# A two-layer diffusion block in fp32 on one core: every operand of a matrix product moved to a multiple of 256 bytes

## The chip, the cores and the metric

The kernel runs on one core of a Trainium2 chip. The metric is the device time of one launch in microseconds (us): 2267.54 us as the median of three runs before the change (2266.43 to 2267.88).

## The reference

A backbone of two layers works on 256 latent tokens and 256 context tokens of width 1024. Each layer is a half-step SwiGLU feed-forward block, then four token mixers on one normalised input (grouped attention, a convolution module, differential attention, a Fourier mix), gated and merged, then a second feed-forward block. In the second layer the context stream stops after the mixers' inputs.

```python
def half_ffn(h, shift, scale, gate, g, w1, w3, w2):
    n = modulate(rms_norm(h, g), shift, scale)
    return h + 0.5 * gate * swiglu(n, w1, w3, w2)      # D_FF = 2816
...
for l in range(DEPTH):                                 # DEPTH = 2
    h, hc = half_ffn(h, ...), half_ffn(hc, ...)
    y, y_ctx = token_mixing(n, nc, w_in[l], ...)       # IN_COLS = 7936, W_OUT 1024 x 1024
    h = half_ffn(h + m[:, 5] * y, ...)
    if l < DEPTH - 1:
        hc = half_ffn(hc + mc[:, 5] * y_ctx, ...)
return rms_norm(h, final_g)
```

## The kernel before, in words

Features lie on the 128 partitions and tokens along the free dimension. Latent and context tokens stand side by side, so most products have 512 moving columns; where only the latent stream is left, or where the closing steps take the two streams apart, they have 256.

**Three products for one.** A float32 value is split into a high part of type float32r and the rest, also float32r. `mm3` (L195 to L199) forms one block of a product from three matmuls: weight high by activation high (L197), weight high by activation low (L198), weight low by activation high (L199). In every one the weight block of 128 x 128 is the stationary operand (a weight load, LDWEIGHTS, precedes each matmul) and the activation is the moving one. Only L908 to L910 have it the other way round. The activations are `nh`, `nl` (the normalised input, 8 blocks of 512 columns), `gh`, `gl` (the hidden layer of the feed-forward block, 22 blocks), `yh`, `yl` (the mixers' outputs), and in the attention `kk` and `sq` tiles (L828, L829), which are float32r too. The weights are `hi` and `lo`, cut by `cut` on ScalarE (L182) and VectorE (L183) out of a `raw` chunk of 512 KB, eight blocks, which SyncE's queue loads. A few products keep plain float32 operands: the transposes (L368, L379, L844, L865), the attention's values (L889, L949), the Fourier mix (L757, L768, L769), the modulation (L257, L303). The built program has 11,388 float32r matmuls, 6,452 with 512 columns and 4,936 with 256, and 928 float32 ones.

**Stages.** `run` (L1079 on) goes through the start (`start`, with its own pool `first`), then for each layer `ffn`, `mixing`, `ffn`. In `ffn` the "up" products come first (22 x 2 columns of weights, moving `nh` and `nl`), then the "down" products (moving `gh` and `gl`): six of eight output blocks with 512 columns (L197 to L199, tiles `pr`), the last two stream by stream with 256 columns in `close` (tiles `pr` and `prc`), where the weights of the very last chunks lie in two spare tiles (tiles `w`). In the second layer's last block all down products have 256 columns.

**Where operands lie.** A tile pool places its tiles one after the other, each on a multiple of 32 bytes; pools follow each other in the order in which they are opened: `fix` (for the whole run), `wp` (weights, three buffers each), `tmp` (scratch), then the pool of the stage at hand (`first`, `ffn..`, `mix..`). All partitions have the same layout. So the small tiles at the end of one pool set the place of all that follows. In the program before, `fix` ends with `lam`, `eps` and `zero` (32 bytes each) and `tmp` holds two `rs` tiles and a `warm` tile of 32 bytes; in the mixing pool `cw` has 496 bytes, `qg` and `stat` 32 each. The built program gives these places, as the remainder of the start address by 256, with the float32r matmuls that read them (every row and block of these tiles is 512, 1024 or 2048 bytes long, so all blocks of a tile have its remainder):

| moving operand | its remainder | stationary operand | its remainder | columns | matmuls |
|---|---|---|---|---|---|
| `nh`, `nl`, `yh`, `yl` of layer 0; `hi`, `lo` at L908 to L910 | 64 | `hi`, `lo`; `nh`, `nl` at L908 to L910 | 64 | 512 | 5040 |
| `nh`, `nl` | 64 | `hi`, `lo` | 64 | 256 | 3168 |
| `gh`, `gl` | 160 | `hi`, `lo` | 64 | 512 | 1188 |
| `gh`, `gl` | 160 | `hi`, `lo` | 64 | 256 | 1032 |
| `yh`, `yl` of layer 1 | 192 | `hi`, `lo` | 64 | 256 | 384 |
| `gh`, `gl` | 160 | spare tiles (`w`) | 160 | 256 | 288 |
| `kk` (attention keys) | 192 | `sq` (queries) | 192 | 512 and 256 | 192 |
| `nh`, `nl` | 64 | `hi`, `lo` in pool `first` (the start) | 160 | 512 | 96 |

Each engine goes through its instructions in the order in which they were written or scheduled; the engines wait for each other by semaphores.

Of the kernel before, what the change touches and what calls it, by code (L numbers as in the profile page):

```python
# [10 lines left out]
F32 = mybir.dt.float32  # L11
# [7 lines left out]
L, D, FF = 2, 1024, 2816  # L19
DB, FB = D // 128, FF // 128  # L20
# [4 lines left out]
TAPS = 31  # L25
# [82 lines left out]
class Chunk:  # L108
    def __init__(self, hi, lo):
        self.hi, self.lo = hi, lo  # L110
# [8 lines left out]
class Build:  # L119
    def __init__(self, nc, tc, es, d):  # L120
        self.nc, self.tc, self.d = nc, tc, d
        self.order = []
        self.after = self.region = None
        pool = lambda name, **kw: es.enter_context(tc.tile_pool(name=name, **kw))
        self.fix = pool("fix", bufs=1)
        self.wp = pool("wp", bufs=3)
        self.tmp = pool("tmp", bufs=2)
        self.ps = pool("ps", bufs=1, space=PSUM)
        self.dram = pool("dram", bufs=1, space=bass.MemoryType.DRAM)
        f = self.fix  # L130
        self.small = f.tile([128, N_SMALL], F32, name="small")
        self.const = f.tile([128, EARLY], F32, name="const")
        self.h = f.tile([128, DB, 2 * T], F32, name="h")
        self.nh = f.tile([128, DB, 2 * T], F32R, name="nh")
        self.nl = f.tile([128, DB, 2 * T], F32R, name="nl")
        self.st = f.tile([128, DB, 32], F32, name="st")
        self.mod = [f.tile([128, 72, 2], F32, name=f"mod{l}") for l in range(L)]
        self.lam = [f.tile([128, 4], F32, name=f"lam{l}") for l in range(L)]
        self.eps = f.tile([128, 1], F32, name="eps")
        self.zero = f.tile([128, 1], F32, name="zero")  # L140

    def sm(self, *key):
        o, w = SMALL[key if len(key) > 1 else key[0]]
# [215 lines left out]
    def rstd(self, x, n, count, name, heads=1):  # L359

        nc = self.nc
        ps = self.aux(f"{name}_ps")
        nt = n // 128
        m = nt * heads
        for i in range(nt):
            nc.tensor.transpose(ps[:, 128 * i:128 * i + 128], x[:, 128 * i:128 * i + 128], self.cst("ident"))  # L368
        r = self.tmp.tile([128, 8], F32, tag="rs", name=f"{name}_s", bufs=2)
        nc.vector.tensor_reduce(out=r[:, 0:m], in_=ps[:, 0:n].rearrange("p (m f) -> p m f", m=m), axis=AX.X, op=ALU.add)  # L370
        nc.scalar.activation(out=r[:, 0:m], in_=r[:, 0:m], func=AF.Sqrt, scale=1.0 / count, bias=self.eps)
        nc.vector.reciprocal(out=r[:, 0:m], in_=r[:, 0:m])
        w = self.tmp.tile([128, 512], F32, tag="rstd", name=f"{name}_w", bufs=1)
        nc.vector.tensor_copy(out=w[:, 0:n].rearrange("p (m f) -> p m f", m=m),
                              in_=r[:, 0:m].unsqueeze(2).broadcast_to([128, m, n // m]))

        def turn(ps=ps):
            for i in range(nt):
                nc.tensor.transpose(ps[:, 128 * i:128 * i + 128], w[:, 128 * i:128 * i + 128], self.cst("ident"))  # L379
            return ps[:, 0:n]  # L380

        return turn
# [64 lines left out]
    def project(self, l, m, b, block, n, x, w, h0=None, warm=False):  # L447

        p = self.acc(f"pr{l}{m}{b}")
        for k in range(n):  # L450
            self.mm3(p[:, 0:w], block(b, k), [t[:, 0:w] for t in x(k)], k == 0, k == n - 1)
            if k == n - 1:
                self.epilogue(l, m, b, p, slice(0, w), h0)()
                if warm:
                    t = self.tmp.tile([128, 1], F32, tag="warm", name="warm", bufs=1)
                    self.nc.scalar.activation(out=t, in_=self.ssum[:, 0:1], func=AF.Sqrt)
            if k % 8 == 7 or k == n - 1:
                yield
# [178 lines left out]
    def mixing(self, l, closing):  # L637
# [5 lines left out]
        with self.tc.tile_pool(name=f"mix{l}", bufs=2) as mp:  # L643
            tl = lambda tag, name, bufs, shape=(128, 512), dt=F32: mp.tile(list(shape), dt, tag=tag, name=name,
                                                                            bufs=bufs)
# [20 lines left out]
                return p  # L666


            cw = tl("cw", "cw", 1, (128, 4, TAPS))
            nc.vector.tensor_scalar(out=cw, in0=self.sm("conv_w", l).rearrange("p (i k) -> p i k", k=TAPS),  # L670
                                    scalar1=0.5, scalar2=None, op0=ALU.mult)
            conv_out = [tl(f"cv{i}", f"cv{i}", 1, (128, S, T)) for i in range(4)]
# [150 lines left out]
            def scores(sq, kt, qt, name):  # L823
                keys = ALL if qt < 2 else CTX
                nk = keys.stop - keys.start
                qs = slice(128 * qt, 128 * qt + 128)
                p = self.aux(f"s{name}")
                nc.tensor.matmul(p[:, 0:nk], sq[:, qs], kt[0][:, keys], start=True, stop=False)  # L828
                nc.tensor.matmul(p[:, 0:nk], sq[:, qs], kt[1][:, keys], start=False, stop=True)  # L829
                st = tl("stat", f"st{name}", 4, (128, 2))  # L830
                nc.vector.tensor_reduce(out=st[:, 0:1], in_=p[:, 0:nk], axis=AX.X, op=ALU.max, negate=True)
                e = tl("e", f"e{name}", 4)
                nc.scalar.activation(out=e[:, 0:nk], in_=p[:, 0:nk], func=AF.Exp, bias=st[:, 0:1],
                                     accum_out=st[:, 1:2])
                nc.vector.reciprocal(out=st[:, 1:2], in_=st[:, 1:2])
                return e, st, nk
# [11 lines left out]


            va = tl("va", "va", 1, (128, 4, 128))  # L850
            qg = tl("qg", "qg", 1, (128, 1))
            nc.vector.tensor_scalar(out=qg, in0=self.sm("qk_g", l)[:, 0:1], scalar1=0.125, scalar2=None, op0=ALU.mult)
            ak, aq, ae, at = [], {}, {}, {}

# [19 lines left out]
            def a_scores(j, qt):  # L874
                for a in range(2):
                    e, st, nk = scores(aq[j][a], ak[a], qt, f"a{j}{qt}{a}")
                    scaled(e, nk, st[:, 1:2])
                    ae[j, qt, a] = e, nk
# [17 lines left out]
            lam = self.lam[l]  # L896
# [32 lines left out]
            def c_scores(h, qt):  # L929
                e0, s0, nk = scores(cq[h][0], ck[h][0], qt, f"c{h}{qt}0")  # L930
                e1, s1, nk = scores(cq[h][1], ck[h][1], qt, f"c{h}{qt}1")
                nc.vector.tensor_tensor(out=s1[:, 1:2], in0=s1[:, 1:2], in1=lam[:, 2:3], op=ALU.mult)
                scaled(e1, nk, s1[:, 1:2])
                nc.vector.scalar_tensor_tensor(out=e0[:, 0:nk], in0=e0[:, 0:nk], scalar=s0[:, 1:2], in1=e1[:, 0:nk],
                                               op0=ALU.mult, op1=ALU.add)
                ce[h, qt] = e0, nk
# [230 lines left out]
```

## Time and profile before

| | |
|---|---|
| three runs: median, lowest, highest | 2267.54, 2266.43, 2267.88 us |
| the profiled execution: its own time | 2266.95 us |
| its span from the first to the last instruction | 2265.2 us |
| mean granted TensorE clock | 0.997 |
| VectorE, ScalarE, GpSimd busy | 65%, 43%, 5% of the span |
| 16 DMA engines: hardware queue's share | 42.4%; 322.81 MB in all, mean 143 GB/s |

PE is TensorE's matmul row, PEld its weight loads, DVE VectorE, ACT ScalarE, POOL GpSimd, SP SyncE. A matmul's row has its start and its length; since matmuls are pipelined and their ends are modelled, the next one starts before that length is over. The distance between two starts is therefore what a matmul costs where TensorE has no other wait, and it is read from the times at which the rows start.

### The profile page before, as it was taken

What the parts mean: (1) busy time and instruction counts of PE and PEld (TensorE: products, weight loads), DVE (VectorE), ACT (ScalarE), POOL (GpSimd) and SP (SyncE); (2) the same over time, 40 slices, a digit from 0 to 9 for tenths busy, and PEclk for the clock granted to TensorE, in tenths of its full rate; (3) what the DMA queues carried; (4) which work ended last, traced back from release to release, by engine and by line L of the source; (5) the groups of instructions that cost most, each with busy time, mean ns of one, the idle gap of its engine ahead of it and who ended that gap; (6) DMA issues with size and microseconds to landing.
All of it is one profiled execution on the core that took longest, in us unless ns stands there. A gap on an engine that the chain in (4) does not pass through costs nothing.

```text
span 2265.2 us, 32288 instructions
## 1 busy us (share of the span) xinstructions
PE 2216.1 (98%) x12822; PEld 1915.5 (85%) x12822; DVE 1479.9 (65%) x2432; ACT 964.6 (43%) x1513; POOL 117.7 (5%) x124
## 2 busy tenths in 40 slices
PE   6999999999999999999999999999999999999998
PEld 4888889888888788888888898888889898998998
DVE  6788874794778645556565545665537889775554
ACT  4323223455557633342222232223224777754443
POOL 0000000000000112110000010000001000121000
PEclk9999999999999999999999999999999999999999
DMA  8566663311222232334544424454534333454553
GB/s 323 184 202 202 207 214 117 119 66 65 75 75 75 75 103 93 112 112 153 163 161 156 155 82 145 158 167 149 165 115 170 122 121 122 139 181 164 180 184 131
DMA packets 92742, 322.81 MB, mean 143 GB/s; under 512 B 9904, under 2 KB 15280, under 8 KB 91952
## 3 DMA queue, kind: packets, MB, share of 16 engines
q1 hardware_dynamic: 92592, 320.76, 42.4%
q8 instruction: 100, 1.64, 0.3%
q14 instruction: 50, 0.41, 0.1%
HBM read 315.48 MB, written 5.24 MB: 142 GB/s over the span
## 4 chain that ended last, share of the span: by engine, by line
PE 87%; DVE 9%; ACT 3%; issue 1%; DMA 0%; POOL 0%; DVEq 0%; SPq 0%; ACTq 0%; POOLq 0%
PE p L198 12%; PE p L199 12%; PE p L197 12%; PE pr L199 7%; PE pr L198 6%; PE pr L197 6%; PE g L197 3%; PE g L198 3%; PE g L199 3%; DVE cv L699 2%; DVE lo L183 2%; PE b L197 2%; PE b L198 2%; PE b L199 2%; PE ao L889 1%
## 5 line engine op out<-in xcount | busy, mean ns | idle before, releaser
L182 ACT ACTIVATE hi<-raw 128x1024 fp32r<-128x1024 f32 x430 | 454.6, 1058 | 885.7 <-issue 250.1
L183 DVE TENSOR_TENSOR lo<-raw,hi 128x1024 fp32r<-128x1024 f32 x422 | 526.2, 1248 | 293.1 <-ACT hi L182 286.9
L197 PE MATMUL p<-nh,hi 128*128 128x512 f32 (+1 forms) x1456 | 521.7, 358 | 2.4 <-ACT nh L409 1.3
L199 PE MATMUL p<-nh,lo 128*128 128x512 f32 (+1 forms) x1456 | 520.9, 358 | 2.5 <-DVE lo L183 2.5
L198 PE MATMUL p<-nl,hi 128*128 128x512 f32 (+1 forms) x1456 | 521.2, 358 | 1.2 <-DVE nl L416 1.1
L325 DVE SCALAR_TENSOR_TENSOR prods<-raw,cond 128x1024 f32<-128x1024 f32 x240 | 289.1, 1222 | 191.5 <-DMA raw<-wst 188.6
L197 PEld LDWEIGHTS p<-nh,hi 128*128 128x128 f32 x1456 | 276.6, 190 | 43.8 <-ACT nh L409 2.2
L199 PEld LDWEIGHTS p<-nh,lo 128*128 128x128 f32 x1456 | 276.6, 190 | 42.9 <-DVE lo L183 3.7
L198 PEld LDWEIGHTS p<-nl,hi 128*128 128x128 f32 x1456 | 276.6, 190 | 41.5 <-DVE nl L416 2.1
L199 PE MATMUL pr<-gh,lo 128*128 128x512 f32 (+1 forms) x656 | 231.4, 353 | 0.0
L198 PE MATMUL pr<-gl,hi 128*128 128x512 f32 (+1 forms) x656 | 229.4, 350 | 0.0
L197 PE MATMUL pr<-gh,hi 128*128 128x512 f32 (+1 forms) x656 | 228.4, 348 | 0.0
L197 PE MATMUL g<-nh,hi 128*128 128x512 f32 (+1 forms) x512 | 174.9, 342 | 0.0
L199 PE MATMUL g<-nh,lo 128*128 128x512 f32 (+1 forms) x512 | 173.4, 339 | 0.0
L198 PE MATMUL g<-nl,hi 128*128 128x512 f32 (+1 forms) x512 | 172.6, 337 | 0.0
L699 DVE SCALAR_TENSOR_TENSOR cv<-yp,cw,cv 128x512 f32<-128x512 f32 (+1 forms) x240 | 148.7, 620 | 4.8
L198 PEld LDWEIGHTS pr<-gl,hi 128*128 128x128 f32 x656 | 123.2, 188 | 19.4
L197 PEld LDWEIGHTS pr<-gh,hi 128*128 128x128 f32 x656 | 123.6, 188 | 18.0
L199 PEld LDWEIGHTS pr<-gh,lo 128*128 128x128 f32 x656 | 123.1, 188 | 17.0
L197 PEld LDWEIGHTS g<-nh,hi 128*128 128x128 f32 x512 | 97.0, 189 | 10.5 <-issue 0.6
L199 PEld LDWEIGHTS g<-nh,lo 128*128 128x128 f32 x512 | 97.0, 189 | 10.4 <-issue 0.2
L198 PEld LDWEIGHTS g<-nl,hi 128*128 128x128 f32 x512 | 97.0, 190 | 9.9 <-issue 0.2
(427 smaller groups left out, 3415.7 us busy)
## 6 DMA issues: line engine op xcount, KB each, us to landing
raw<-wst SPq DMA_DIRECT2D x556, 512.0 KB, 3.4
adaraw<-wst SPq DMA_DIRECT2D x3, 2048.0 KB, 17.1
adaraw<-wst SPq DMA_DIRECT2D x8, 512.0 KB, 7.4
cond<-cond SPq DMA_DIRECT2D x3, 1024.0 KB, 4.8
h<-h SPq DMA_DIRECT2D x2, 1024.0 KB, 7.9
adaraw<-wst SPq DMA_DIRECT2D x2, 1024.0 KB, 10.6
parked<-h SPq DMA_DIRECT2D x8, 256.0 KB, 3.9
h<-parked SPq DMA_DIRECT2D x8, 256.0 KB, 3.1
```

The lines of the kernel that those rows point to most:

```text
L182: self.nc.scalar.activation(out=hv, in_=r, func=AF.Copy)
L183: getattr(self.nc, low).tensor_tensor(out=lv, in0=r, in1=hv.bitcast(F32), op=ALU.subtract)
L197: mm(out, w[0], x[0], start=start, stop=False)
L198: mm(out, w[0], x[1], start=False, stop=False)
L199: mm(out, w[1], x[0], start=False, stop=stop)
L325: nc.vector.scalar_tensor_tensor(out=products[:, s], in0=r, scalar=1.0, in1=cond[:, s], op0=ALU.mult, op1=ALU.mult, accum_out=self.mod[l][ ...
L699: nc.vector.scalar_tensor_tensor(out=o, in0=x, scalar=wk, in1=o, op0=ALU.mult, op1=ALU.add)
L889: nc.tensor.matmul(o[64 * a:64 * a + 64, 0:128], va[:, k0 + k, 64 * a:64 * a + 64], at[j, qt][a][:, 128 * k:128 * k + 128], start=k == 0, ...
```

## The change

Sizes and places of tiles alone. A pool `tiny` is opened ahead of `fix` and takes the `rs` and `warm` tiles; the two loops over dummy tiles only fix their order. In `fix` the small tiles come first, `zero` is widened to 128 bytes, and with them in front `const`, `st`, `h`, `nh` and `nl` begin on multiples of 256 bytes. In the mixing pool `cw`, `stat` and `qg` are widened to 512, 64 and 256 bytes (four `stat` tiles make 256), and views of the old size are used.

In the built program after the change every float32r operand in the table above, moving and stationary, has the remainder 0; so have the float32 operands of the other products, but for every other block of `st`, whose blocks are 128 bytes long (remainder 128). The number, order and shape of the instructions on every engine, and every semaphore that they wait for or raise, are those of before: both programs have the same 18,608 instructions, apart from the addresses. The scratch and raw tiles move with the others (for instance `raw` from 64 to 0, `temp` tiles from 128 to 0). Line numbers grow by 4 from `sm` on.

```diff
         pool = lambda name, **kw: es.enter_context(tc.tile_pool(name=name, **kw))
+        self.tiny = pool("tiny", bufs=1)
         self.fix = pool("fix", bufs=1)
...
         f = self.fix
+        for i in range(2):
+            self.tiny.tile([128, 8], F32, tag="rs", name=f"rs{i}", bufs=2)
+        self.tiny.tile([128, 1], F32, tag="warm", name="warm", bufs=1)
+        self.lam = [f.tile([128, 4], F32, name=f"lam{l}") for l in range(L)]
+        self.eps = f.tile([128, 1], F32, name="eps")
         self.small = f.tile([128, N_SMALL], F32, name="small")
+        self.mod = [f.tile([128, 72, 2], F32, name=f"mod{l}") for l in range(L)]
+        self.zero = f.tile([128, 32], F32, name="zero")[:, 0:1]
         self.const = f.tile([128, EARLY], F32, name="const")
+        self.st = f.tile([128, DB, 32], F32, name="st")
         self.h = f.tile([128, DB, 2 * T], F32, name="h")
         self.nh = f.tile([128, DB, 2 * T], F32R, name="nh")
         self.nl = f.tile([128, DB, 2 * T], F32R, name="nl")
-        self.st = f.tile([128, DB, 32], F32, name="st")
-        self.mod = [f.tile([128, 72, 2], F32, name=f"mod{l}") for l in range(L)]
-        self.lam = [f.tile([128, 4], F32, name=f"lam{l}") for l in range(L)]
-        self.eps = f.tile([128, 1], F32, name="eps")
-        self.zero = f.tile([128, 1], F32, name="zero")
...
-        r = self.tmp.tile([128, 8], F32, tag="rs", name=f"{name}_s", bufs=2)
+        r = self.tiny.tile([128, 8], F32, tag="rs", name=f"{name}_s", bufs=2)
...
-                    t = self.tmp.tile([128, 1], F32, tag="warm", name="warm", bufs=1)
+                    t = self.tiny.tile([128, 1], F32, tag="warm", name="warm", bufs=1)
...
-            cw = tl("cw", "cw", 1, (128, 4, TAPS))
+            cw = tl("cw", "cw", 1, (128, 4 * TAPS + 4))[:, 0:4 * TAPS].rearrange("p (i k) -> p i k", k=TAPS)
...
-                st = tl("stat", f"st{name}", 4, (128, 2))
+                st = tl("stat", f"st{name}", 4, (128, 16))[:, 0:2]
...
-            qg = tl("qg", "qg", 1, (128, 1))
+            qg = tl("qg", "qg", 1, (128, 64))[:, 0:1]
```

## The prediction

> **What bounds the kernel now.** I read the page's busy times first, then the chain of work that ended last, then PE's waits, and then the distances between the starts of matmuls in the timeline.
>
> ```profile
> PE 2216.1 (98%) x12822; PEld 1915.5 (85%) x12822; DVE 1479.9 (65%) x2432; ACT 964.6 (43%) x1513; POOL 117.7 (5%) x124
> ...
> PE 87%; DVE 9%; ACT 3%; issue 1%; DMA 0%; POOL 0%; DVEq 0%; SPq 0%; ACTq 0%; POOLq 0%
> ...
> PE n_ps L368 <- DVE ssum L248: 18.1, 2, 13.2
> PE n_ps L379 <- DVE n_w L374: 3.6, 5, 1.3
> ```
>
> TensorE is busy 98% of the span and makes 87% of the chain. Its longest waits are at the start (18.1 us for the first sums of squares); all others together are some 24 us. So the time is the sum over the matmuls, each at its distance to the next start. The change touches addresses alone, so the question is whether that distance depends on where operands lie. The trace of before holds a natural experiment: the feed-forward block's up and down products have the same shapes, but the moving operand lies at 64 in one and at 160 in the other (remainders by 256, from the table above). This is the first block of layer 1, up products, then down products:
>
> ```profile
> L197 PE MATMUL p<-nh,hi 128*128 128x512 f32 x328 | 127.6, 389 | 0.0
> L198 PE MATMUL p<-nl,hi 128*128 128x512 f32 x328 | 127.6, 389 | 0.0
> L199 PE MATMUL p<-nh,lo 128*128 128x512 f32 x328 | 127.6, 389 | 0.0
> ...
> 1360.57 0.40 PE L197 MATMUL p<-nh,hi 128*128 128x512 f32 x1
> ...
> 1583.41 0.39 PE L199 MATMUL p<-nh,lo 128*128 128x512 f32 x1
> 1583.63 0.40 PE L197 MATMUL pr<-gh,hi 128*128 128x512 f32 x1
> ...
> 1675.81 0.40 PE L199 MATMUL pr<-gh,lo 128*128 128x512 f32 x1
> ...
> L199 PE MATMUL pr<-gh,lo 128*128 128x512 f32 x132 | 52.7, 399 | 0.0
> L198 PE MATMUL pr<-gl,hi 128*128 128x512 f32 x132 | 52.0, 394 | 0.0
> L197 PE MATMUL pr<-gh,hi 128*128 128x512 f32 x132 | 51.8, 392 | 0.0
> ```
>
> Both stretches are free of waits (last column 0.0). Up: 3 x 328 = 984 matmuls from 1360.57 to 1583.41, 222.84 us over 983 distances, **226.7 ns** each. Down: 396 matmuls from 1583.63 to 1675.81, 92.18 over 395, **233.4 ns** each. The weights lie at 64 in both. So 6.7 ns of a down matmul come with a moving operand at 160 beside a weight block at 64. Row by row the down distances repeat with the triple:
>
> ```profile
> 320.40 0.39 PE L197 MATMUL pr<-gh,hi 128*128 128x512 f32 x1
> 320.63 0.39 PE L198 MATMUL pr<-gl,hi 128*128 128x512 f32 x1
> 320.87 0.40 PE L199 MATMUL pr<-gh,lo 128*128 128x512 f32 x1
> 321.10 0.39 PE L197 MATMUL pr<-gh,hi 128*128 128x512 f32 x1
> ```
>
> Three matmuls take 0.70 us, 233.3 ns each, the third (0.87 to 1.10, then on) as dear as the others: a rate, not one stall. Now 256 columns:
>
> ```profile
> 1331.02 0.28 PE L197 MATMUL prc<-gh,w 128*128 128x256 f32 x1
> ...
> 1333.42 0.28 PE L199 MATMUL prc<-gh,w 128*128 128x256 f32 x1
> ...
> 2190.54 0.28 PE L198 MATMUL p<-nl,hi 128*128 128x256 f32 x1
> 2190.66 0.28 PE L199 MATMUL p<-nh,lo 128*128 128x256 f32 x1
> ...
> 2191.14 0.28 PE L197 MATMUL pr<-gh,hi 128*128 128x256 f32 x1
> ...
> 2254.37 0.28 PE L199 MATMUL pr<-gh,lo 128*128 128x256 f32 x1
> ...
> L198 PE MATMUL pr<-gl,hi 128*128 128x256 f32 x176 | 49.8, 283 | 0.0
> L199 PE MATMUL pr<-gh,lo 128*128 128x256 f32 x176 | 49.7, 282 | 0.0
> ```
>
> The first pair spans 20 distances with both operands at 160: 2.40 us, 120.0 ns. The last pair spans 528 matmuls (three groups of 176) with 160 beside 64: 63.23 us over 527, also 120.0. The two rows in between, at 64 beside 64, are 0.12 apart. With 256 columns the place doesn't count in any pair that occurs.
>
> From 226.7 at 512 columns and 120.0 at 256 a column costs 106.7 / 256 = 0.417 ns, so a fixed part of 13.3 ns stands on top of the columns (226.7 - 213.3), and 20.0 in the down products. The 6.7 is the difference of two rates that I can see; whether the 13.3 has to do with place too is the large unknown of this change, since no float32r operand lies at 0 or 128 now.
>
> What speaks to it is the attention in the mixing, where moving and stationary operand lie at 192 together, with a stretch at 64 and 64 on both sides:
>
> ```profile
> 650.64 0.39 PE L198 MATMUL bg<-nl,hi 128*128 128x512 f32 x1
> 650.87 0.40 PE L199 MATMUL bg<-nh,lo 128*128 128x512 f32 x1
> 651.10 0.39 PE L828 MATMUL sc<-ck0h,cq 128*128 128x512 f32 x1
> 651.33 0.39 PE L829 MATMUL sc<-ck0l,cq 128*128 128x512 f32 x1
> 651.56 0.39 PE L828 MATMUL sc<-ck0h,cq 128*128 128x512 f32 x1
> 651.78 0.40 PE L829 MATMUL sc<-ck0l,cq 128*128 128x512 f32 x1
> 652.02 0.39 PE L197 MATMUL ba<-nh,hi 128*128 128x512 f32 x1
> 652.25 0.39 PE L198 MATMUL ba<-nl,hi 128*128 128x512 f32 x1
> 652.47 0.39 PE L199 MATMUL ba<-nh,lo 128*128 128x512 f32 x1
> ```
>
> From 650.87 to 652.25 there are six distances, 1.38 us, some 20 ns more than six times 226.7, for one way in (64 to 192) and one way out. Between the two, from 651.33 to 651.78, it is 0.45 for two distances: the old rate. So 192 beside 192 runs like 64 beside 64, and the price falls due where the places differ. I read this as two streams, the running matmul's and the next weights', that fit together when both start at the same place and disturb each other when they don't. Then only the difference of the places counts, and after the change it is zero everywhere.
>
> **The change part by part.** Instructions, order and waits are those of before; nothing is added.
>
> 1. *`gh`, `gl` from 160 to 0, weights from 64 to 0, 512 columns.* 3 x 396 = 1188 matmuls in three blocks, at 233.4 - 226.7 = 6.7 ns: **8.0 us**. All of it on PE without a wait. What would be late next is the weights:
>
> ```profile
> 0.00:56.00 56.00, 36.09 (x425) 27.59 (x426) 34.74 (x70) 25.09 (x33) 0.20 (x4) 1.00 0.87 326
> 273.50:365.90 92.40, 92.40 (x397) 74.33 (x396) 63.68 (x95) 23.34 (x25) 0.00 (x0) 1.00 0.63 205
> ```
>
> In the first such stretch, the second line here (columns: window, length, PE, PEld, DVE, ACT, POOL, clock, DMA share, GB/s; the first line is the start, used below), VectorE is busy 63.7 of 92.4 us, ScalarE 23.3, the DMAs 63%: 2.7 us less per stretch uncovers nothing.
>
> 2. *The changes of place in the mixing go.* The program has 102 neighbours among float32r matmuls whose places differ; at 20 ns for a pair of them, and nothing at 256 columns, between 0 and 1.0 us. I take **0.7**, near the row above.
>
> 3. *The start, `nh` at 64 beside weights at 160.* 96 matmuls; if each pays the same 6.7 ns it is 0.6 us, but PE waits there for ScalarE and VectorE (18.1 us above), and a faster matmul before a wait gains nothing. Between 0 and 0.6; I take **0.3**.
>
> 4. *256 columns*: 4936 matmuls at 120.0 at every pair of places. Nothing.
>
> 5. *ScalarE's, VectorE's and GpSimd's operands and the DMAs' targets* move by 64 to 128 bytes. No row shows a price of place there. They lie beside PE, except at the start and the end; the DMAs' part at the start is bounded by its 87% share in the first 56 us, and a percent of these would be 0.5 us. I take 0, and up to 1 us either way.
>
> Sum: 8.0 + 0.7 + 0.3 = 9.0 us. Against the profiled execution, 2266.95 us (1.75 more than its span of 2265.2), that is **2258.0 us**; the median, 2267.54, lies 0.6 above that execution.
>
> The Trainium skill, "TensorE: Matmul & The Clock Gate", section "Step-by-step: what each phase is for", says that TensorE has two independent read ports and that loading the next weights takes no read bandwidth from the running matmul. By that rule the place of one operand against the other could not matter, and the sum would be 0. The trace differs, 233.4 against 226.7 ns.
>
> **The rivals.**
>
> *A: the fixed 13.3 ns is a price of place too.* If each operand read that doesn't begin on a large enough boundary costs extra, 64, 160 and 192 all pay and only 0 would not. For it: 13.3 ns is 32 columns' time, 128 bytes, exactly what a read shifted by 64 would touch more if memory were read in pieces of 128 bytes, at both widths. Against it: under such a price 160 and 64 should cost the same with 512 columns, and 64, 160 and 192 behave alike only when paired alike. At most it frees 11,388 x 13.3 = 152 us, and 8 for the first step: 2107. Half of it, for instance at one of the widths, gives 2267 - 76 - 8 = 2183. VectorE's 63.7 us in 92.4 leaves room for that. The same page of the Trainium skill, section "Wait — 56ns, not 53.3ns?", gives a floor of about 2.5 ns above the columns for back-to-back matmuls; worked out as an estimate from it, 10.8 x 11,388 + 8 makes 2136, and no row here has reached that floor at this rate.
>
> *B: no change.* The 6.7 ns belong to `gh` and `gl` for another reason (their distance from each other, the order of buffers) and stay. For it: only one pair of long 512-column stretches shows them. Against it: the attention's rows, and the start at 64 beside 160, where undisturbed distances are as long:
>
> ```profile
> 55.15 0.39 PE L197 MATMUL p<-nh,hi 128*128 128x512 f32 x1
> 55.38 0.40 PE L198 MATMUL p<-nl,hi 128*128 128x512 f32 x1
> 55.62 0.39 PE L199 MATMUL p<-nh,lo 128*128 128x512 f32 x1
> ```
>
> (0.47 us for two, 235 each, with the moving operand at 64 and the weights at 160.) It gives 2267.
>
> *C: slower.* With everything at 0, both streams of every matmul start in the same piece of memory. If that is a bad meeting where 64 and 64 was a good one, the 5040 matmuls that now run at 226.7 pay what the down products pay, 6.7 ns: 34 us, 2301. It decides as soon as the common place costs them 9.0 us / 5040 = 1.8 ns each. For it: place 0 is untested. Against it: 64, 160 and 192, each paired with itself, cost the same.
>
> **How the numbers follow.** Forecast 0.73, A 0.14, B 0.08, C 0.05. About 0.2%, 4.5 us, is what a measurement here can tell from no change: faster means under 2263.0. The forecast with all its bounds lies between 2267 - 8.0 - 1.0 - 0.6 - 1 = 2256 and 2267 - 8.0 + 1 = 2260; I widen it to 2252 to 2262 for what I didn't see of the steps after float32 products. The range takes in B, up to 2268: 0.73 + 0.08 = 0.81. Faster 0.73 + 0.14 less a little for a smaller gain, 0.86; same 0.09; slower 0.05.
>
> **What would show it.** In the down products the three groups should come to 389 ns of length (from 399, 394 and 392) and distances of 226.7, their 396 matmuls to 89.8 us; up products should stay at 226.7, and 256 columns at 120.0. The distances around the attention should lose their 0.23 to 0.24. If the up products' distances shrink, A holds, and the forecast's reading of the fixed part is wrong; if they grow, C; if the down products keep 233, B.

## The result

| | before | after |
|---|---|---|
| median of 5 runs (lowest to highest), us | 2267.54 (2266.43 to 2267.95) | 2259.19 (2257.51 to 2261.28) |
| ratio of the times, 95% interval | | 0.9964 (0.995 to 0.9979) |
| profiled execution, its span, us | 2266.95, 2265.2 | 2257.51, 2255.7 |

The kernel got faster by 8.35 us in the medians and by 9.4 in the profiled executions. 2258.0 had been predicted, between 2252 and 2268. In another set of runs on one chip the changed kernel came to 2258.6 against 2265.64, a ratio of 0.9969 (0.9958 to 0.9981).

First the page of the changed kernel (busy times and the chain) and PE's longest wait, in the places of those shown of before:

```profile
PE 2206.8 (98%) x12822; PEld 1915.0 (85%) x12822; DVE 1478.4 (66%) x2432; ACT 964.2 (43%) x1513; POOL 117.4 (5%) x124
...
PE 87%; DVE 8%; ACT 3%; issue 1%; DMA 0%; POOL 0%; DVEq 0%; SPq 0%; ACTq 0%; POOLq 0%
...
PE n_ps L372 <- DVE ssum L252: 17.7, 2, 12.8
```

TensorE's busy time went from 2216.1 to 2206.8 us, 9.3 less, with the same 12,822 matmul rows (a float32 product can have two). The waits stand where they stood, and VectorE's and ScalarE's busy times changed by 1.5 and 0.4 us. So what was gained lies in the matmuls' own rate.

The changed kernel's timeline, PE alone, at the edges of the up and the down products of the first block of layer 1:

```profile
1352.36 0.40 PE L201 MATMUL p<-nh,hi 128*128 128x512 f32 x1
...
1575.20 0.39 PE L203 MATMUL p<-nh,lo 128*128 128x512 f32 x1
1575.43 0.39 PE L201 MATMUL pr<-gh,hi 128*128 128x512 f32 x1
...
1664.96 0.39 PE L203 MATMUL pr<-gh,lo 128*128 128x512 f32 x1
```

Up: 222.84 us over 983 distances, 226.7 ns, as before. Down: 89.53 us over 395, **226.7 ns** where it had been 233.4. Their groups in that window (matmuls alone, each shape apart) have one length now:

```profile
L201 PE MATMUL pr<-gh,hi 128*128 128x512 f32 x132 | 51.3, 389 | 0.0
L202 PE MATMUL pr<-gl,hi 128*128 128x512 f32 x132 | 51.3, 389 | 0.0
L203 PE MATMUL pr<-gh,lo 128*128 128x512 f32 x132 | 51.3, 389 | 0.0
```

389 ns stands in each row, where it had been 392, 394 and 399. Now 256 columns in the changed kernel's timeline: the first and last row of a group of `yh` and `yl` in layer 1's mixing that ran without a wait, then of the last block's down products:

```profile
1974.70 0.28 PE L201 MATMUL b<-yh,hi 128*128 128x256 f32 x1
...
1977.46 0.28 PE L203 MATMUL b<-yh,lo 128*128 128x256 f32 x1
...
2181.24 0.28 PE L201 MATMUL pr<-gh,hi 128*128 128x256 f32 x1
...
2244.47 0.28 PE L203 MATMUL pr<-gh,lo 128*128 128x256 f32 x1
```

and the same `yh` group in the timeline of the kernel before:

```profile
1985.64 0.28 PE L197 MATMUL b<-yh,hi 128*128 128x256 f32 x1
...
1988.38 0.28 PE L199 MATMUL b<-yh,lo 128*128 128x256 f32 x1
```

The last block: 63.23 us over 527 distances, 120.0 ns, as before. The `yh` group (24 matmuls, 23 distances): 2.76 us now, 120.0 each, and 2.74 before, 119. With the moving operand at 192 beside weights at 64 these products had been a little *faster*; being laid alike cost them 1 ns each. This pair stands in the table of places ahead of the prediction, and its rate had not been read.

Matmul by matmul (both profiles have the same 12,822 rows in the same order), the distances between starts changed as follows: the 1188 down products of 512 columns by -7.97 us, the start's products (64 beside 160) by -0.55, `yh` at 256 columns by +0.30, the other products in the first layer's mixing, the attention's among them, by about -0.3; the first matmul started 0.4 earlier. A further -0.6 us is no gain of the change: it comes from stretches at half the granted clock, shown in the last section. The profile of before has one near 980 us that this one lacks (-1.5 us here), while the one near 2050 us is twice as long in this one (+1.0).

### The profile page after: what moved, and what is told of

It is laid out like the page before. It is cut to its first block, busy times and chain, and to the rows that moved or that the text cites. A ratio compares the mean times of both kernels' runs of the same rounds, so it can differ in the third digit from the quotient of the medians.

```text
span 2255.7 us, 32288 instructions
## 1 busy us (share of the span) xinstructions
PE 2206.8 (98%) x12822; PEld 1915.0 (85%) x12822; DVE 1478.4 (66%) x2432; ACT 964.2 (43%) x1513; POOL 117.4 (5%) x124
## 4 chain that ended last, share of the span: by engine, by line
PE 87%; DVE 8%; ACT 3%; issue 1%; DMA 0%; POOL 0%; DVEq 0%; SPq 0%; ACTq 0%; POOLq 0%
PE p L203 12%; PE p L202 12%; PE p L201 12%; PE pr L202 6%; PE pr L203 6%; PE pr L201 6%; PE g L201 3%; PE g L202 3%; PE g L203 3%; DVE cv L703 2%; DVE lo L187 2%; PE b L201 2%; PE b L202 2%; PE b L203 2%; PE ao L893 1%
```

## The experiments

Three theories stood. **S**, the forecast's: two streams, and only the difference between the place of the moving operand and that of the weights (remainders by 256) counts. **P**, rival A: each operand pays for its own place, in pieces of 64 bytes or more. **G**, rival B: the 6.7 ns are the hidden layer's own. In the edits below a tile in front shifts those that follow it.

**1. Both at 64.** The kernel before, with one tile ahead of `gh`, so that `gh`, `gl` and the spare weight tiles move from 160 to 64, where the other weights are. Nothing lies at 0.

```diff
         with self.tc.tile_pool(name=f"ffn{l}{j}", bufs=1) as pool:
+            pool.tile([128, 40], F32, name="pad")
             gh = pool.tile([128, FB, w], F32R, name="gh")
```

> The layout of before with one tile of 160 bytes put ahead of gh in the feed-forward pools: gh, gl and the spare weight tiles lie at 64 instead of 160, beside weights at 64; nothing else moves and nothing is a multiple of 256. Theory S (only the difference between the places of the running matmul's moving operand and of the weights loaded beside it counts): down products with 512 columns at 226.7 ns, 8.0 us less than before, 2259.5. Theory P (each operand pays for its own place where that is no multiple of 64 bytes): the same 226.7 and 2259.5. Rival G (the 6.7 ns belong to gh and gl whatever their place): 233.4 ns, 2267.5. A price that only multiples of 256 are free of: 233.4 ns, 2267.5.

2259.04 us (2256.92 to 2261.89, 7 runs) against 2266.65, ratio 0.9969 (0.9958 to 0.9979). Its timeline, first and last down product of that block:

```profile
1579.74 0.39 PE L197 MATMUL pr<-gh,hi 128*128 128x512 f32 x1
...
1669.28 0.39 PE L199 MATMUL pr<-gh,lo 128*128 128x512 f32 x1
```

89.54 us over 395, 226.7 ns. One tile of 160 bytes does what the whole change does (2259.04 and 2259.19), and no multiple of 256 is needed. G falls: the same buffers in the same order lost the 6.7 ns by a change of place alone. S and P had both foreseen this.

**2 and 3. Six other differences.** The changed kernel, with `gh`, `gl` pushed on by another amount in each feed-forward block; the weights stay at 0. The second of the two has 160, 192, 224 and 128 in place of these four numbers.

```diff
+            pad = {(0, 0): 32, (0, 1): 64, (1, 0): 128, (1, 1): 32}[l, j]
+            pool.tile([128, pad // 4], F32, name="pad")
             gh = pool.tile([128, FB, w], F32R, name="gh")
```

> The changed layout with a tile ahead of gh whose size differs from block to block: gh and gl lie at 32 in the first feed-forward block, at 64 in the second, at 128 in the third, at 32 in the last (256 columns); all weights stay at 0. Theory S: every one of the three 512-column stretches costs more than 226.7 ns, about 230 to 237 as at a difference of 96; the last stays at 120.0. Theory P: 233.3 at 32, 226.7 at 64 and 128. Rival G: 226.7 in all three. Time by S some 2265 to 2267, by P 2261 to 2262.

> As the run before, with gh and gl at 160, 192 and 224 in the first three feed-forward blocks and at 128 in the last; weights at 0. Theory S: all three stretches above 226.7 ns; if the two streams' meeting repeats every 256 bytes, 160, 192 and 224 need not cost what 96, 64 and 32 cost. Theory P: 233.3 at 160 and 224, 226.7 at 192. Rival G: 226.7 in all three.

2261.02 and 2264.79 us, one run each. The timeline of the first, from the first to the last down product of 512 columns of each block (32, 64, 128), and within the 64 block a stretch of 72 matmuls of 256 columns:

```profile
272.47 0.40 PE L201 MATMUL pr<-gh,hi 128*128 128x512 f32 x1
...
364.64 0.40 PE L203 MATMUL pr<-gh,lo 128*128 128x512 f32 x1
...
1213.98 0.40 PE L201 MATMUL pr<-gh,hi 128*128 128x512 f32 x1
...
1304.41 0.39 PE L203 MATMUL pr<-gh,lo 128*128 128x512 f32 x1
...
1328.30 0.28 PE L201 MATMUL prc<-gh,hi 128*128 128x256 f32 x1
...
1336.34 0.28 PE L203 MATMUL prc<-gh,lo 128*128 128x256 f32 x1
...
1577.91 0.40 PE L201 MATMUL pr<-gh,hi 128*128 128x512 f32 x1
...
1670.07 0.39 PE L203 MATMUL pr<-gh,lo 128*128 128x512 f32 x1
```

Over 395 distances: 92.17 us for 32, 233.3 ns; 90.43 for 64, **228.9**; 92.16 for 128, 233.3. The stretch of 256 columns at 64: 8.04 us over 71, **113.3**. The other, 160, 192 and 224:

```profile
274.27 0.40 PE L201 MATMUL pr<-gh,hi 128*128 128x512 f32 x1
...
366.81 0.39 PE L203 MATMUL pr<-gh,lo 128*128 128x512 f32 x1
...
1216.35 0.39 PE L201 MATMUL pr<-gh,hi 128*128 128x512 f32 x1
...
1308.52 0.39 PE L203 MATMUL pr<-gh,lo 128*128 128x512 f32 x1
...
1582.23 0.40 PE L201 MATMUL pr<-gh,hi 128*128 128x512 f32 x1
...
1674.40 0.40 PE L203 MATMUL pr<-gh,lo 128*128 128x512 f32 x1
```

92.54, 92.17 and 92.17 us: 234.3, 233.3 and 233.3 ns. Every difference but 0 and 64 costs 6.6 ns or more. P in pieces of 64 bytes falls, since 128 and 192 are multiples of 64 and pay. S had missed too: it expected 230 to 237 ns at 64 as well, and 2265 to 2267 us for the first of the two runs, which took 2261.02. What neither theory had: at 256 columns every one of these differences was faster than equal places (the table in the last section, from stretches of 72 to 528 matmuls); that gain, 2.5 us, and the cheap block at 64 put the first run below S's time.

**4. Everything at 32.** The changed kernel with one small tile 32 bytes longer, so that all float32r operands lie at 32.

```diff
-        self.zero = f.tile([128, 32], F32, name="zero")[:, 0:1]
+        self.zero = f.tile([128, 40], F32, name="zero")[:, 0:1]
```

> The changed layout with 32 bytes more ahead of const: every operand of a matrix product, moving and stationary, lies at 32, none at a multiple of 64. Theory S: all as in the changed kernel, 226.7 and 120.0 ns, 2258 to 2260. Theory P: every matmul with 512 columns pays 6.7 ns or twice that (moving and weights), 6452 x 6.7 = 43 us or more: 2302 or slower. A price that only multiples of 256 are free of: slower than the changed kernel by at least the 9 us, 2267 or more.

2257.09 us (2255.3 to 2259.22, 5 runs), ratio to the kernel before 0.9958 (0.9944 to 0.9971). Its timeline at the same edges:

```profile
1354.05 0.40 PE L201 MATMUL p<-nh,hi 128*128 128x512 f32 x1
...
1576.89 0.39 PE L203 MATMUL p<-nh,lo 128*128 128x512 f32 x1
1577.12 0.39 PE L201 MATMUL pr<-gh,hi 128*128 128x512 f32 x1
...
1666.65 0.39 PE L203 MATMUL pr<-gh,lo 128*128 128x512 f32 x1
```

222.84 us over 983 and 89.53 over 395: 226.7 ns both. The common place makes no difference, at 32 as at 0 and 64. This ends P as stated here, and rival A, which the unchanged up products had already ruled out, with it.

**5. A difference of 64 nearly everywhere.** The changed kernel with `hi` and `lo` at 192 and the moving operands at 0, so that the difference is 64 again, with other places.

```diff
         self.nl = f.tile([128, DB, 2 * T], F32R, name="nl")
+        self.wp.tile([128, 48], F32, tag="pad", name="pad", bufs=1)
+        self.tmp.tile([128, 16], F32, tag="pad", name="pad2", bufs=1)
```

> The changed layout with hi and lo moved to 192 and everything else left at multiples of 256, so that nearly every matmul reads its moving operand 64 bytes past the weights' place (by 256). Theory S with the map of the runs before: 512 columns at 228.9 instead of 226.7 ns (6132 matmuls, +14 us; the 192 of L912 to L914 at 233.3, +1.3 us), 256 columns at 117.9 instead of 120.0 (some 4600 matmuls, -10 us), or at 113.3 if they settle as in one short stretch of that map (-31 us): between 2241 and 2265. Theory P (each operand pays alone for a place that is no multiple of 64): nothing changes, 2258 to 2260.

2259.05 us (2253.94 to 2260.42, 4 runs), ratio 0.9961 (0.9947 to 0.9974), the changed kernel's time. Its timeline, first and last up product, then the first and the last down product of 512 columns:

```profile
1359.08 0.39 PE L203 MATMUL p<-nh,hi 128*128 128x512 f32 x1
...
1584.08 0.39 PE L205 MATMUL p<-nh,lo 128*128 128x512 f32 x1
1584.31 0.39 PE L203 MATMUL pr<-gh,hi 128*128 128x512 f32 x1
...
1674.72 0.39 PE L205 MATMUL pr<-gh,lo 128*128 128x512 f32 x1
```

225.00 over 983 and 90.41 over 395: 228.9 ns each, the rate that 64 beside 0 had shown. So it is the difference by 256 that counts. At 256 columns it had 117.8 in the long stretches and 113.3 in some short ones. Matmul by matmul against the changed kernel, where no wait interfered, 512 columns lost 13.1 us and 256 columns gained 12.6: they cancel.

**6. Equal places for 512 columns, 64 apart for 256.** What experiments 2 to 5 point to: from the first product of the second layer's mixing on, where nearly all products have 256 columns, `nh` and `nl` are used 64 bytes further on; the last block's `gh`, `gl` and the second mixing's `yh`, `yl` lie at 64; the weights stay at 0. Some small tiles change places to make room.

```diff
+        wide = [f.tile([128, 2 * T * DB + 16], F32R, name="nh")]
...
+        wide.append(f.tile([128, 2 * T * DB + 64], F32R, name="nl"))
+        at = lambda o: [t[:, o:o + 2 * T * DB].rearrange("p (b t) -> p b t", b=DB) for t in wide]
+        (self.nh, self.nl), self.shifted = at(0), at(16)
...
+        if (l2, which) == (1, 1):
+            self.nh, self.nl = self.shifted
...
+            if (l, j) == (1, 1):
+                pool.tile([128, 16], F32, name="pad")
...
+                    if first:
+                        tl("pad1", "pad1", 1, (128, 16))
```

> The changed layout, with a difference of 64 bytes only where the products have 256 columns: in the second layer nh and nl are used 16 columns further on from the mixing's first product to the end (2592 matmuls with 256 columns), gh and gl of the last block lie at 64 (528), and so do yh and yl of the second mixing (384); weights stay at 0, and the 512-column products of the other stages keep equal places. Theory S: 3504 matmuls gain 2.1 ns (7.5 us) or, settled as in the short stretch, 6.7 ns (23 us), and 192 with 512 columns lose 2.3 to 6.7 ns (0.9 us): 2251 down to 2236, faster than the changed kernel. If the gain of the map was an accident of two short stretches: 2258 to 2260.

2251.78 us (2251.08 to 2254.78, 5 runs), ratio to the kernel before 0.9936 (0.9922 to 0.995). Run again on one chip with the changed kernel:

> The kernel with a difference of 64 bytes in the second layer's 256-column products once more, beside the changed kernel on the same chip. Theory S with the measured 117.8 ns for 3504 matmuls: 6 to 8 us below the changed kernel, 2250 to 2254. If its lead was the chip's: the same time as the changed kernel.

> The changed kernel itself, on the chip and beside the runs of the kernel before that the next kernel has too. Theory S as before: 2257 to 2261, 512 columns at 226.7, 256 at 120.0 ns. If the drop of the first measurement were one chip's or one session's: nearer to 2267.

2251.14 us (2250.64 to 2253.29) beside 2258.6 (2256.29 to 2260.91): 7.5 us faster than the changed kernel, 14.5 than the kernel before. The timeline of this kernel's first profiled execution (2251.08 us), the last block's down products:

```profile
2176.40 0.28 PE L204 MATMUL pr<-gh,hi 128*128 128x256 f32 x1
...
2238.47 0.28 PE L206 MATMUL pr<-gh,lo 128*128 128x256 f32 x1
```

62.07 us over 527, 117.8 ns, where equal places gave 63.23. Matmul by matmul between the two profiled executions on one chip, the 3,383 products of 256 columns that no wait disturbed got 7.6 us shorter, 2.25 ns each, and the 192 of 512 columns that use the shifted `nh`, `nl` (half of them as the stationary operand) paid 0.8. So some 6.8 of the 7.5 us are shown to be the places'. The rest need not be: the changed kernel's profile has three stretches at half the clock there and this one's has one.

**7. A smaller weight load.** Is the fixed 13.3 ns of an equally laid matmul the price of the load beside it? The changed kernel with half the weight columns in the second product, which halves that load.

```diff
-        mm(out, w[0], x[1], start=False, stop=False)
+        mm(out[0:64], w[0][:, 0:64], x[1], start=False, stop=False)
```

> The changed kernel with the second product of each three (weight high by activation low) cut to the first 64 of its 128 stationary columns: that part of the product is left out for the upper 64 outputs. Its weight load reads 256 bytes instead of 512, while the first product runs. If the fixed 13.3 ns is time that the weight load takes from the running matmul: the distance from the first product to the second falls by some 6.7 ns (to 220 at 512 columns), the other two stay at 226.7, or the same share in the sum of the three. If it is a cost of changing weights or of starting a matmul: all three stay at 226.7.

2263.11 us, one run. The loads of the down products by group, and the timeline of the down products of 512 and of 256 columns:

```profile
L201 PEld LDWEIGHTS pr<-gh,hi 128*128 128x128 f32 x656 | 123.1, 188 | 17.1
...
L202 PEld LDWEIGHTS pr<-gl,hi 128*64 128x64 f32 x656 | 88.7, 135 | 16.9
```

```profile
1589.79 0.39 PE L201 MATMUL pr<-gh,hi 128*128 128x512 f32 x1
...
1680.55 0.39 PE L203 MATMUL pr<-gh,lo 128*128 128x512 f32 x1
...
2189.03 0.28 PE L201 MATMUL pr<-gh,hi 128*128 128x256 f32 x1
...
2250.51 0.28 PE L203 MATMUL pr<-gh,lo 128*128 128x256 f32 x1
```

The load got shorter, 135 ns from 188. The matmuls of 512 columns got *slower*: 90.76 us over 395, 229.8 ns; those of 256 faster: 61.48 over 527, 116.7. Both expectations missed the 512 columns. By product the distances of 512 columns were 228.9, 230.4 and 230.0 ns, so the first did not fall and the others did not stay. Where no wait interfered, 512 columns lost some 17 us in all and 256 gained some 14, which is how the time came out above the changed kernel's. So the fixed part is not in proportion to the load. The edit also halves the output rows of the second product, so which of the two made 512 columns slower isn't shown.

**8. One of the two weight tiles aside.** Which load disturbs which matmul? The changed kernel with `lo` alone at 96 and all else at 0, so that one of the three products meets another difference, 160 by 256 (0 less 96).

```diff
+                if not self.padded and pool is None:
+                    self.padded = self.wp.tile([128, 24], F32, tag="pad", name="pad", bufs=1)
                 lo = (pool or self.wp).tile([128, 8, 128], F32R, tag="lo", name=f"lo{i}", bufs=bufs)
```

> The changed layout with lo alone moved to 96; hi and all moving operands stay at 0. Theory S (running matmul against the weights loaded beside it): the distance from the second product to the third grows, since lo is loaded while the second runs; over the three the mean rises by a third to all of 6.7 ns. If what counts is a matmul's own pair of operands: the distance from the third product to the next first grows. If neither, 226.7 in all.

2286.48 us, one run. Its timeline, the down products of 512 columns:

```profile
1604.72 0.40 PE L205 MATMUL pr<-gh,hi 128*128 128x512 f32 x1
...
1696.59 0.39 PE L207 MATMUL pr<-gh,lo 128*128 128x512 f32 x1
```

91.87 us over 395, 232.6 ns, against 226.7; the 528 of 256 columns in the last block came to 119.0. The rise is not confined to one matmul in three: by line the distances after the three products are 233.3, 231.7 and 232.8. The mean rose by 5.9 ns, within what S allowed, but all three distances grew where each theory had named one. This experiment doesn't tell whether a matmul is disturbed by the weights for itself or by those for the next; it shows that one ill-placed operand in three slows the whole stream. That made this the slowest kernel of the study: against the changed kernel the products of 512 columns lost 33.8 us, and those of 256 gained 3.8.

## Why the prediction was right

- **Term 1, the down products, 8.0 us.** Right in cause and size: 7.97 us measured, 233.4 to 226.7 ns. Experiment 1 gets it with these places alone changed. Nothing was late behind them; the columns 0.0 say that no wait was uncovered.
- **"Only the difference of the places counts."** Shown for 512 columns: equal places at 0, at 32 and at 64 all give 226.7; 64 beside 0 and 0 beside 192 both give 228.9. Two more differences were met from two places each: 160 as 160 beside 0 (experiment 3, 234.3) and as 64 beside 160 (the start of the kernel before, 234.2 over 81 undisturbed distances); 192 as 192 beside 0 (experiment 3) and as 0 beside 64 (experiment 6), 233.3 both. The price is no single one, though: 2.2 ns at 64, 6.6 to 7.6 elsewhere.
- **"The running matmul's and the next weights'" streams disturb each other.** Not shown. In most stretches a matmul's own weights and the next ones have the same place; experiment 8 sets them apart and all three distances rose, and with half a load (experiment 7) the distance beside it did not get shorter at 512 columns.
- **Term 2, the mixing, 0.7 us.** Too large: some 0.3 in the whole of the first layer's mixing. The changed kernel's timeline at the attention:

```profile
646.95 0.39 PE L203 MATMUL bg<-nh,lo 128*128 128x512 f32 x1
647.17 0.39 PE L832 MATMUL sc<-ck0h,cq 128*128 128x512 f32 x1
...
648.08 0.39 PE L201 MATMUL ba<-nh,hi 128*128 128x512 f32 x1
648.30 0.39 PE L202 MATMUL ba<-nl,hi 128*128 128x512 f32 x1
```

Six distances are 1.35 us, where 1.38 had been, so the mechanism is there; but most of the 102 neighbours stood at a wait or had 256 columns, and the price of one place doesn't hold for all.
- **Term 3, the start, 0.3 us.** 0.55 measured, near the upper bound of 0.6: of its 96 matmuls, 82 had distances below 250 ns before and after, and they lost 6.5 ns each, 0.53 us. The wait for ScalarE and VectorE was not what set them.
- **Term 4, "with 256 columns the place doesn't count in any pair that occurs": wrong.** `yh` at 192 beside 64 had 119 ns, and lost 0.30 us by the change. The reading took two pairs for all. That it stayed small is luck: equal places, which the change makes universal, are the dearest or tied for it at 256 columns.
- **Term 5, the other engines.** VectorE's and ScalarE's busy times changed by 0.1% of their own or less; nothing of it shows in the time.
- **The sum.** 9.0 us predicted, 9.4 between the profiled executions, 8.35 between the medians, 7.0 in the second set of runs. The terms measured make 7.97 + 0.3 + 0.55 - 0.30 = 8.5; the rest of the profiled 9.4 is the first matmul's earlier start, 0.4, and the stretches at half the clock, 0.6. Term 1 carries the forecast. The small terms, 1.0 us foreseen and 0.55 measured, were each off, in part against each other.
- **The rivals.** A fell to the up products, unchanged at 226.7, and to experiment 4; B to experiment 1; C's "place 0 is untested" to the same 226.7.

The Trainium skill, "TensorE: Matmul & The Clock Gate", section "Step-by-step: what each phase is for", has the weight load take no read bandwidth from the running matmul, with independent ports. If that meant that the operands' places can't matter to each other, these runs would not agree: the same matmuls take 226.7 or 233.3 ns by the place of one operand against the other. Whether it is read bandwidth that is lost, no run here shows.

## What to carry to other kernels

Where float32r matmuls follow each other without a wait, read the distance between their starts against the start addresses of the moving operand and of the weights, by their remainders by 256: the difference decides, the common value doesn't. That is shown for float32r with a 128 x 128 load for every matmul and places that are multiples of 32; other types were not tried. In this kernel equal remainders were best for 512 columns. For 256, a difference of 64 beat equal ones by 2.2 ns, and the stretches at 32, 160 and 192 were about as good; a whole kernel was timed at 64 alone. One tile of padding (experiment 1) was worth 7.6 us of 2267. A change that is said to need alignment may need only equality, and one experiment with everything at an odd common place (32 here) tells the two apart.

## What was not expected of the hardware

**A map that turns over with the width.** Distances in ns by the difference (moving operand less weights, by 256), float32r, 128 x 128 weights loaded for every matmul:

| difference | 0 | 32 | 64 | 96 | 128 | 160 | 192 | 224 |
|---|---|---|---|---|---|---|---|---|
| 512 columns | 226.7 | 233.3 | 228.9 | 233.4 | 233.3 | 234.3 | 233.3 | 233.3 |
| 256 columns | 120.0 | 116.7 to 117.8 | 113.3 or 117.8 | 120.0 | 118.6 | 117.3 | 113.8 or 117.8 | 118.3 |

(96 is the kernel before.) At a difference of 64, 256 columns have two rhythms: 113.3 in some stretches of up to 103 matmuls, 117.8 in the long ones. At 192 one stretch of 24 came to 113.8. Which one a stretch falls into was not controlled, and it changes between executions of one program: 40 products near 2037 us took 113.3 ns in experiment 6 and 117.8 in its repetition; if the 113.3 could be held in the last block alone, it would save another 528 x 4.5 ns = 2.4 us.

**The fixed part's cause stays open.** Equal places leave 13.3 ns on top of the columns' time. It is not a price of the common place (the same at 0, 32 and 64) and not in proportion to the load (7), and it is not always there: 113.3 is only 6.7 above the 106.7 of 256 columns. It also vanishes at half the clock. Windows of before and of after that hold the same matmuls (TensorE's granted clock is the seventh column), and the timeline of before in that window:

```profile
977.47:984.13 6.66, 5.39 (x33) 5.19 (x32) 5.54 (x13) 2.57 (x6) 2.92 (x3) 0.74 0.50 176
```

```profile
973.34:978.52 5.18, 3.90 (x33) 3.69 (x32) 4.62 (x10) 1.48 (x4) 2.19 (x2) 1.00 0.68 229
```

```profile
980.74 0.41 PE L198 MATMUL p<-nl,hi 128*128 128x256 f32 x1
...
981.80 0.41 PE L197 MATMUL p<-nh,hi 128*128 128x256 f32 x1
```

A granted clock of 0.74 over 6.66 us is some 3.4 us at half. Five distances of 256 columns there are 1.06 us, 212 ns each (213 in the finer starts), twice the 106.7 with nothing on top. The Trainium skill, the same page, section "Wait — 56ns, not 53.3ns?", states this: the fixed cost of a matmul shows only at the full clock. The trace agrees on that; on its size, about 2.5 ns there, it does not, since the least that a stretch shows here is 6.7. Such stretches stand near 980, 1780 and 2055 us, one to three of them in each of the twelve profiles, 3.4 or 6.8 us long. Each has 5 to 28 distances that are too long, by 93 ns at 256 columns and 200 at 512, and costs 0.6 to 2.4 us. They follow waits: in the 3.4 us ahead of the three in the profile of before TensorE was busy for 1.58, 1.44 and 1.15 us. They may account for a good part of the 2 us by which runs of one kernel differ: of experiment 1's seven executions, the three with a mean granted clock of 0.994 took 2261.75 to 2261.89 us, the four with 0.997 took 2256.92 to 2259.04.
